# A hybrid attention and RWKV-7 backbone: the next front's VectorE work behind the transposes of the running inversion, and two modulation units made in another stage

## The chip, the core and the metric

The kernel runs on one core of one Trainium2 chip. Its engines are TensorE (PE; PEld is its weight load), VectorE (DVE), ScalarE (ACT), GpSimd (POOL) and SyncE (SP, whose queue issues the DMAs here). The metric is the device time of one launch in microseconds (us), as the median of several runs; beside it there is one execution taken by the hardware profiler, from which all rows below come.

## The reference

Two layers over a trunk of 256 context tokens and 512 latent tokens, 1024 features, in float32. Every sub-layer is normalised, and shifted, scaled and gated by vectors that a linear map makes out of SiLU(c) for latent tokens and SiLU(c_ctx) for context tokens (adaLN):

```
sh1, sc1, gt1, sh2, sc2, gt2 = split(silu_c @ ada_w[i] + ada_b[i], 6)    # and the same of silu_cc
h = rmsnorm(x, norm1_g[i]) * (1 + sc1) + sh1
x = x + gt1 * mixer(h)
x = x + gt2 * relu(modulate(rmsnorm(x), sh2, sc2) @ w1)**2 @ w2
```

Layer 0 mixes by windowed grouped-query attention with context keys, a sink per head, QK-norm and rotary positions. Layer 1 mixes by RWKV-7: out of the shifted tokens come r, k, v, a decay w per direction, and a, b; then a generalized delta rule runs over the tokens, forward and backward, 16 heads of 64:

```
S_t = S_{t-1} diag(w_t) + (S_{t-1} a_t) b_t^T + v_t k_t^T ;   y_t = S_t r_t
```

The latent scans start from the last context state of their direction. A group norm, a bonus and a gate per direction, and an output projection follow; then the second MLP.

## The kernel before

**Order of work.** The program is traced stage by stage: setup, attention, MLP of layer 0, features of layer 1, scan, MLP of layer 1. A planner then orders each engine's instructions: it simulates the engines with a cost model and hands each the ready instruction that was traced first. So work that is traced later can stand earlier in an engine's queue when it was ready sooner by the model. On the chip every queue is in order. `issue_after(ins)` adds an edge without a wait: the instructions traced under it, on the engine of `ins`, stand behind `ins` in that engine's queue. Other engines and the DMAs are not bound by it. Loads and stores are all issued by SP.

**adaLN units.** `ada` holds 12 units (six per layer) of 1024 features. A unit is made in two halves (`ada_parts`): eight loads of 128x512 weights (256 KB each), for each four small matmuls (each recorded as two, so 64 records a half) into one PSUM tile of tag "a", then a copy by ACT, a transpose by PE and an addition of the bias by DVE. A half is two parts of four loads. Four halves (units 0 and 1) are made at the start. The other ten units are a list `fill`; in the attention's loop over (head group `gq`, query tile `qt`) two parts of it follow each `attend`, but for four places where a query projection stands instead.

**Features of layer 1** (`rwkv_features`). The tiles hp, xx and kt are placed where the first MLP's tiles stood. DVE makes the normalised tokens (L780), their neighbours' sum (L785) and the mix tiles (L839, L846); PE projects keys out of them (`k_ps`), and row m of `kt` is written when projection m is done. `wtile` loads a weight (L349) and splits it in a high part (ACT or POOL, L330 and L332) and a low part (DVE, L333). `side_weights` does the same with the small matrices; its first loads are the `swr` ones.

**Scan.** The tokens are cut in chunks of 64. Six iterations stand in a list `its`: 0 and 3 are context (four feature tiles of two heads), 1, 2, 4 and 5 latent (two feature tiles). Each goes through these steps:

- `prep(it)`: loads of the features (rings f4 of five buffers, cs of two, en of one), two exponentials by ACT (L1182 and L1183; L1159 and L1160 for context), three or four products by DVE for each feature tile and direction (a "part": L1195, L1196, L1197, L1199), a copy by POOL (L1200), and half of the Gram matrices (`grams`: copies into `pad` by ACT, matmuls L1220, mask by DVE L1226).
- `lanes(it)`: the inversion of the triangular matrices, by 32x32 blocks. Four copies into MT, the transpose L1267, and then 30 dependent steps of products and sums on DVE (L1277, L1280).
- `merge(it)`: the transposes L1285 and L1288 on DVE end the inversion; four copies into GM follow (L1249 on DVE, L1245 on ACT), and two rounds of small matmuls with copies between them (L1295, L1298, L1303, L1306).
- `chain(it)`: the recurrence over the chunks on PE, ACT and DVE (x_ps, u_ps, s_ps, y_ps; DVE's state update is L1405). Its values come by `values` into two z tiles (loads L1337).
- `late(it)`: the other half of the Grams, products by the chunk's decay (L1241) and transposes (L1319), a piece after a chain step.
- `readout(it)`: group norm and gates (L1441 to L1475), a piece after a step of the next chain. Its buffers come from the rings f4 and cs, too.

`front(n)` traces `merge(its[n-1])`, `prep(its[n])` and `lanes(its[n])`. Front 1 comes ahead of the first chain and front n+2 behind chain n. Iterations n and n+2 share one set of AR, BK and GM, so prep(n+2) can write when chain n has read.

Of the kernel before, what the change touches and what calls it, by code (L numbers as in the profile page):

```python
# [1 line left out]

# [6 lines left out]
F32 = mybir.dt.float32  # L9
# [10 lines left out]
P = 128  # L20
# [120 lines left out]
LC = (0, 2, 4, 4)  # L141
NCS = 2
NEN = 1
M0 = 0
SQ = ()
LM = ()
LPRE = 0
# [1 line left out]
TPER = 3  # L149
TPRE = 0  # L150
S1 = 6
AP_ = 2
S3 = 24
C1 = (20,)
C3 = 3
# [13 lines left out]
class K:  # L169
# [46 lines left out]
        self.ada = self.cp.tile([P, 12, 8, 2], F32, name="ada")  # L216


    def ada_parts(self, pool, u, i, tag="adaw", bufs=4, after=None):

        nc = self.nc
        st = {}

        def part(q):
            if q == 0:
                st["ps"] = self.ps.tile([P, 512], F32, tag="a", name="ada_ps")
            ps = st["ps"]
            for k in range(4 * q, 4 * q + 4):
                w = pool.tile([P, 512], F32, tag=tag, bufs=bufs, name="ada_w")
                with self.tc.issue_after(after) if after else ExitStack():  # L230
                    self.last_ada = nc.sync.dma_start(w, self.a["ada_w"][u, i, k]).ins
                for j in range(4):
                    nc.tensor.matmul(ps[32 * j:32 * j + 32, 0:P], self.sil[:, k, :], w[:, P * j:P * j + P],
                                     start=(k == 0), stop=(k == 7), tile_position=(0, 32 * j))
            if q == 0:
                return
            sb = pool.tile([P, P], F32, tag="ada_sb", bufs=2, name="ada_sb")
            nc.scalar.activation(sb, ps[:, 0:P], AF.Copy)
            pt = self.ps.tile([P, 512], F32, tag="a", name="ada_pt")[:, 0:P]
            nc.tensor.transpose(pt, sb, self.ident)  # L240
            f = 8 * u + 4 * i
            nc.vector.tensor_tensor(self.ada[:, u, 4 * i:4 * i + 4], pt.rearrange("p (j x) -> p j x", x=32)[:, :, 0:2],
                                    self.v["ada_b"][:, f:f + 4].unsqueeze(2).to_broadcast([P, 4, 2]), ALU.add)

        return [lambda q=q: part(q) for q in range(2)]
# [145 lines left out]
    def attention(self):  # L391
# [21 lines left out]
        self.sil = rp.tile([P, 8, 32], F32, name="sil")  # L413
        nc.vector.memset(self.sil, 0.0)
        nc.scalar.activation(self.sil[:, :, 0:2], self.cv, AF.Silu)
        wk = []
        for i in range(2):
            for u in (1, 0):
# [6 lines left out]
        first_ada = self.last_ada  # L425
# [170 lines left out]
            query(m)  # L596
        OS = [None] * 4

        fill = [p for u in range(2, 12) for i in range(2) for p in self.ada_parts(rp, u, i, after=first_ada)]
        late = {(0, 1): 4, (0, 3): 5, (1, 3): 6, (1, 5): 7}  # L600
        X = None
        for gq in range(4):
            if gq < 2:
                OS[gq] = slot(f"O{gq}")
            elif gq == 2:
                both = ap.tile([P, 8, T], F32R, tag="hh", name="O23")
                OS[2:4] = [both[:, 0:4], both[:, 4:8]]
                X = self.open_x()
                for k in range(0, 8, 2):
                    nc.sync.dma_start(X[:, k:k + 2], a["xT"][:, k:k + 2])  # L610
            for qt in range(6):
                attend(gq, qt, OS[gq])
                if (gq, qt) in late:
                    query(late[gq, qt])
                else:
                    for _ in range(AP_):
                        if fill:
                            fill.pop(0)()
        for p in fill:
            p()  # L620
        rstack.close()
# [127 lines left out]
    def rwkv_features(self, xs, scan):  # L749
# [64 lines left out]
        def side_weights(src):  # L814

            hi = rp.tile([P, 1024], F32R, tag="swh", name="swh")
            lo = rp.tile([P, 1024], F32R, tag="swl", name="swl")
            for i in range(2):
                c = slice(512 * i, 512 * i + 512)
                raw = tmp(512, "swr")  # L820
                nc.sync.dma_start(raw, src[:, c])
                self.split(raw, hi[:, c], lo[:, c])
            return hi, lo
# [2 lines left out]
        bsel = rload("bsel", F32R).rearrange("p (f m) -> p f m", f=8)  # L826
        cen = rload("cen")
        w_lo = side_weights(a["lw1"])

        def mix_tile(m, k, xh, xl, lat=False, first=False):  # L830
            sl = ML if lat else slice(0, NM)
# [231 lines left out]
    def rwkv_scan(self, xsave, osave):  # L1063
# [174 lines left out]
        def to_end(it, fl, d):  # L1238

            x = it.BK[:, d, fl * it.nch:fl * it.nch + it.nch]  # L1240
            nc.vector.tensor_tensor(x, x, it.PC[:, ::1 - 2 * d, fl, d].unsqueeze(2).to_broadcast([P, it.nch, P]), ALU.mult)  # L1241
# [40 lines left out]
        def merge(it):  # L1282
# [2 lines left out]
            nc.vector.transpose(MT.rearrange("p u i -> p i u"), Lt.rearrange("p t s -> p s t"))  # L1285

            DT = dt if it.n else GM[:, 0, :, 64:96]
            nc.vector.transpose(DT.rearrange("p u t -> p t u"), lane)  # L1288
            R = [slice(64 * d, 64 * d + 32) for d in range(2)]
            Q = [slice(64 * d + 32, 64 * d + 64) for d in range(2)]  # L1290
            for u0 in (0, 16):
# [212 lines left out]
            if nx:  # L1504
                values(*nx)

        yield prep(its[0]) + [lambda fl=fl, d=d: to_end(its[0], fl, d) for fl in range(4) for d in range(2)] + [lambda: turn(its[0]), lambda: lanes(its[0])] + ([lambda: merge(its[0])] if M0 else [])

        self.pst.close()
        self.wst.close()  # L1510
# [21 lines left out]
            return [state[f // 2][:, 0:1], state[f // 2][:, 1:2]]  # L1532

        def front(n):
            if n > M0:
                merge(its[n - 1])
            for p in prep(its[n]):
                p()
            lanes(its[n])
            rest.extend(late(its[n]))  # L1540
            for _ in range(LPRE):
                if rest:
                    rest.pop(0)()
# [215 lines left out]
```

## Time and profile before

| | |
|---|---|
| median of 3 runs | 2294.5 us (2293.07 to 2295.82) |
| the profiled execution | 2292.35 us, of which the span of the trace is 2290.6 us |
| mean granted TensorE clock | 0.931 |
| busy share | PE 90%, PEld 73%, DVE 58%, ACT 37%, POOL 12% |
| stages, roughly | attention's loop to 412 us, its output projection and the MLP of layer 0 to 1029, features to 1375, scan to 1918, MLP of layer 1 to the end |

A row of groups holds: line, engine, operation, tiles (out <- in), shapes, count | busy us, mean ns of one | idle us of the engine just ahead of them, and what ended it. A row of the timeline holds: start, length, engine, line, operation, tiles, count [idle ahead <- what ended it]. A row of waits: who <- whom: total us, times, longest. A row of a table by stretch: from:to, length, then for each engine its busy us (count of instructions), then the granted clock, the share of the DMA engines and GB/s.

### The profile page before, as it was taken

Reading aid. Unit: us, or ns where it says so; the run is one execution under the profiler, and the core shown is the slowest. Engines: PE = TensorE matmul, PEld = TensorE weight load, DVE = VectorE, ACT = ScalarE, POOL = GpSimd, SP = SyncE. Lnnn points to the kernel's source line nnn. Section 1 sums busy time; section 2 is a strip of 40 time slices with the busy share of each in tenths; the row PEclk is TensorE's granted clock in tenths of the full one; section 3 lists DMA queues with packets and bytes.
Section 4 is the critical chain, followed back from the end, with each engine's and each line's share of the span. In section 5 each row is a group of like instructions: output and inputs, shape, how many; then the busy total and the mean of one; then the engine's idle time right before and its main releaser. Section 6 shows DMA issues by size and latency. Waiting matters only on the chain. (4 is left out here: it accounts for less than half of the span.)

```text
span 2290.6 us, 40501 instructions
## 1 busy us (share of the span) xinstructions
PE 2051.4 (90%) x16208; PEld 1669.3 (73%) x16208; DVE 1317.8 (58%) x2736; ACT 857.9 (37%) x1702; POOL 280.5 (12%) x360
## 2 busy tenths in 40 slices
PE   5989999979999999995989798499568896999999
PEld 4876756868888888884867687387457664788887
DVE  4455564363334343349687575888787757445444
ACT  4354454232111111116454446467556543222121
POOL 0122232010000000003010101000110101110110
PEclk8999999989999999997989898698688897999999
DMA  8244465221212122112246434203310312333322
GB/s 292 94 143 141 153 205 158 74 74 65 65 60 65 56 69 61 55 36 90 76 175 226 129 125 155 61 23 95 104 58 14 126 57 74 102 92 99 95 92 79
DMA packets 115886, 229.67 MB, mean 100 GB/s; under 512 B 12913, under 2 KB 31089, under 8 KB 115313
## 3 DMA queue, kind: packets, MB, share of 16 engines
q1 hardware_dynamic: 115696, 227.08, 30.9%
q8 instruction: 128, 2.10, 0.4%
q14 instruction: 62, 0.50, 0.1%
HBM read 191.80 MB, written 32.60 MB: 98 GB/s over the span
## 5 line engine op out<-in xcount | busy, mean ns | idle before, releaser
L333 DVE TENSOR_TENSOR wlo<-wraw,whi 128x1024 fp32r<-128x1024 f32 (+1 forms) x121 | 134.1, 1116 | 322.7 <-ACT whi L330 170.4
L358 PE MATMUL w_ps<-mhh,whi 128*128 128x512 f32 (+1 forms) x768 | 236.0, 362 | 7.3 <-POOL whi L332 4.0
L360 PE MATMUL w_ps<-mhl,whi 128*128 128x512 f32 (+1 forms) x768 | 236.4, 362 | 6.1 <-DVE mhl L313 6.1
L362 PE MATMUL w_ps<-mhh,wlo 128*128 128x512 f32 (+1 forms) x768 | 236.1, 362 | 6.2 <-DVE wlo L333 6.2
L362 PE MATMUL w_ps<-hid,w2l 128*128 128x512 f32 (+1 forms) x768 | 234.0, 359 | 0.0
L360 PE MATMUL w_ps<-hid,w2h 128*128 128x512 f32 (+1 forms) x768 | 231.1, 355 | 0.0
L358 PE MATMUL w_ps<-hid,w2h 128*128 128x512 f32 (+1 forms) x768 | 231.1, 355 | 0.0
L330 ACT ACTIVATE w2h<-w2raw 128x512 fp32r<-128x512 f32 x64 | 40.4, 632 | 329.9 <-PE w_ps L360 297.9
L332 POOL TENSOR_SCALAR whi<-wraw 128x1024 fp32r<-128x1024 f32 (+1 forms) x60 | 70.0, 1167 | 675.0 <-PE w_ps L360 252.9
L654 DVE SCALAR_TENSOR_TENSOR X<-w_ps,ada,X 128x256 f32<-128x256 f32 (+1 forms) x128 | 73.1, 613 | 137.6 <-PE w_ps L362 137.6
L362 PEld LDWEIGHTS w_ps<-mhh,wlo 128*128 128x128 f32 x768 | 128.1, 190 | 32.7 <-DVE wlo L333 9.4
L358 PEld LDWEIGHTS w_ps<-mhh,whi 128*128 128x128 f32 x768 | 128.2, 190 | 31.9 <-POOL whi L332 4.8
L360 PEld LDWEIGHTS w_ps<-mhl,whi 128*128 128x128 f32 x768 | 128.1, 190 | 32.1 <-DVE mhl L313 8.7
L358 PEld LDWEIGHTS w_ps<-hid,w2h 128*128 128x128 f32 x768 | 127.4, 189 | 23.3
L330 ACT ACTIVATE whi<-wraw 128x1024 fp32r<-128x1024 f32 (+1 forms) x61 | 59.1, 968 | 224.7 <-PE w_ps L360 103.8
L362 PEld LDWEIGHTS w_ps<-hid,w2l 128*128 128x128 f32 x768 | 126.5, 188 | 20.8
L360 PEld LDWEIGHTS w_ps<-hid,w2h 128*128 128x128 f32 x768 | 125.5, 188 | 21.9
L683 ACT ACTIVATE mrelu<-w_ps 128x768 f32<-128x768 f32 (+1 forms) x64 | 44.5, 697 | 190.4 <-PE w_ps L362 190.3
L1220 PE MATMUL g_ps<-pad,bk 128*128 128x128 f32 x640 | 96.6, 301 | 3.3 <-ACT pad L1217 2.4
L332 POOL TENSOR_SCALAR w2h<-w2raw 128x512 fp32r<-128x512 f32 x64 | 42.0, 657 | 426.2 <-PE w_ps L360 326.7
L559 DVE CUSTOM_DVE_ANT_0 sm<-sc_ps,consts,vecs 128x256 f32<-128x256 f32 (+2 forms) x96 | 71.7, 760 | 39.1 <-PE pt_ps L580 19.9
L1220 PEld LDWEIGHTS g_ps<-pad,bk 128*128 128x128 f32 x640 | 83.5, 206 | 12.0 <-ACT pad L1217 5.6
(373 smaller groups left out, 4554.1 us busy)
## 6 DMA issues: line engine op xcount, KB each, us to landing
ada_w<-ada_w SPq DMA_DIRECT2D x192, 256.0 KB, 3.6
wraw<-w SPq DMA_DIRECT2D x64, 512.0 KB, 3.2
w2raw<-w SPq DMA_DIRECT2D x128, 256.0 KB, 2.6
feat<-cs SPq DMA_DIRECT2D x16, 390.0 KB, 2.4
cs<-feat SPq DMA_DIRECT2D x24, 260.0 KB, 2.9
wraw<-wq SPq DMA_DIRECT2D x8, 512.0 KB, 3.6
wraw<-wo SPq DMA_DIRECT2D x8, 512.0 KB, 3.2
wraw<-wkv SPq DMA_DIRECT2D x8, 512.0 KB, 3.3
```

Of the source, the lines that this page charges most:

```text
L330: nc.scalar.activation(hi, raw, AF.Copy)
L332: nc.gpsimd.tensor_scalar(hi, raw, 1.0, 0.0, ALU.mult, ALU.add)
L333: nc.vector.tensor_tensor(lo, raw, hi.bitcast(F32), ALU.subtract)
L358: nc.tensor.matmul(o, wh, cut(xh, sl), start=start, stop=False)
L360: nc.tensor.matmul(o, wh, cut(xl, sl), start=False, stop=False)
L362: nc.tensor.matmul(o, wl, cut(xh, sl), start=False, stop=stop)
L559: nc.vector.tensor_tensor_reduce(sm[:, :nk], ps[:, :nk], self.c["band"][:, b0:b0 + nk], rs[:, h:h + 1], self.v["sink"][:, hd:hd + 1], ALU. ...
L654: self.nc.vector.scalar_tensor_tensor(self.X[:, m, sl], ps[:, sl], self.ada[:, u, m, s:s + 1], self.X[:, m, sl], ALU.mult, ALU.add)
L683: nc.scalar.activation(r, ps[:, 0:n], AF.Relu)
L1220: nc.tensor.matmul(g[:, P * k:P * k + P], it.BK[:, d, b + k], pv[:, :, k], start=True, stop=True)
```

## The change

1. `merge` keeps its second transpose (L1288) as `it.back`. `front(n)` traces `prep(its[n])` under `issue_after(its[n-1].back)`: all DVE instructions of prep(n) stand behind that transpose on DVE's queue. Its loads, its exponentials on ACT, its POOL copies and its matmuls are not bound.
2. Units 8 and 9 (gate 1 and shift 2 of layer 1) leave `fill` and are made in `rwkv_features`, behind the first `side_weights`, ahead of the first mix. Their weights go through nine buffers that are cut out of `kt[:, 1:7]`, their `sil` and their copies stand in `kt[:, 7]`, and POOL writes that `sil` (a memset and a copy). For this, DVE copies SiLU(c) back into `cv` at the start.
3. The remaining 32 parts of `fill` are spread evenly over the 20 places of the attention's loop (12 times two, then 8 times one).
4. Constants that were not used otherwise (M0 of zero, AP_) go.

```
-    def ada_parts(self, pool, u, i, tag="adaw", bufs=4, after=None):
+    def ada_parts(self, pool, u, i, tag="adaw", bufs=4, after=None, home=None):
+        sil = home[0] if home else self.sil
...
-                w = pool.tile([P, 512], F32, tag=tag, bufs=bufs, name="ada_w")
+                w = next(home[1]) if home else pool.tile([P, 512], F32, tag=tag, bufs=bufs, name="ada_w")
...
-            sb = pool.tile([P, P], F32, tag="ada_sb", bufs=2, name="ada_sb")
+            sb = next(home[2]) if home else pool.tile([P, P], F32, tag="ada_sb", bufs=2, name="ada_sb")
...
+        nc.vector.tensor_copy(self.cv, self.sil[:, :, 0:2])
...
-        fill = [p for u in range(2, 12) for i in range(2) for p in self.ada_parts(rp, u, i, after=first_ada)]
+        fill = [p for u in EARLY for i in range(2) for p in self.ada_parts(rp, u, i, after=first_ada)]
+        steps = 24 - len(late)
...
-                    for _ in range(AP_):
-                        if fill:
-                            fill.pop(0)()
+                    steps -= 1
+                    for _ in range(-(-len(fill) // (steps + 1))):
+                        fill.pop(0)()
...
         w_lo = side_weights(a["lw1"])
+        sil = kt[:, 7, 0:256].rearrange("p (k x) -> p k x", k=8)
+        nc.gpsimd.memset(sil, 0.0)
+        nc.gpsimd.tensor_copy(sil[:, :, 0:2], self.cv)
+        wsl = kt[:, 1:7].rearrange("p a t -> p (a t)")
+        home = (sil, itertools.cycle([wsl[:, 512 * i:512 * i + 512] for i in range(9)]),
+                itertools.cycle([kt[:, 7, 256 + P * i:256 + P * i + P] for i in range(2)]))
+        for u in LATER:
+            for i in range(2):
+                for p in self.ada_parts(None, u, i, home=home):
+                    p()
...
-            nc.vector.transpose(DT.rearrange("p u t -> p t u"), lane)
+            it.back = nc.vector.transpose(DT.rearrange("p u t -> p t u"), lane).ins
...
         def front(n):
-            if n > M0:
-                merge(its[n - 1])
-            for p in prep(its[n]):
-                p()
+            merge(its[n - 1])
+            with tc.issue_after(its[n - 1].back):
+                for p in prep(its[n]):
+                    p()
             lanes(its[n])
```

with EARLY = (2, 3, 4, 5, 6, 7, 10, 11) and LATER = (8, 9).

More of the change, by code (lines that the diff above doesn't have):

```diff
@@ L1 @@
+import itertools
 from contextlib import ExitStack
@@ L143 @@
 NEN = 1
-M0 = 0
 SQ = ()
@@ L151 @@
 S1 = 6
-AP_ = 2
+EARLY = (2, 3, 4, 5, 6, 7, 10, 11)
+LATER = (8, 9)
 S3 = 24
@@ L232, in part @@
                 for j in range(4):
-                    nc.tensor.matmul(ps[32 * j:32 * j + 32, 0:P], self.sil[:, k, :], w[:, P * j:P * j + P],
+                    nc.tensor.matmul(ps[32 * j:32 * j + 32, 0:P], sil[:, k, :], w[:, P * j:P * j + P],
                                      start=(k == 0), stop=(k == 7), tile_position=(0, 32 * j))
@@ L1505, in lookahead @@
                 values(*nx)
-        yield prep(its[0]) + [lambda fl=fl, d=d: to_end(its[0], fl, d) for fl in range(4) for d in range(2)] + [lambda: turn(its[0]), lambda: lanes(its[0])] + ([lambda: merge(its[0])] if M0 else [])
+        yield prep(its[0]) + [lambda fl=fl, d=d: to_end(its[0], fl, d) for fl in range(4) for d in range(2)] + [lambda: turn(its[0]), lambda: lanes(its[0])]
         self.pst.close()
```

## The prediction

> **What bounds the kernel now.** First the 40 slices of 57 us, to find where TensorE is not full:
>
> ```profile
> PE   5989999979999999995989798499568896999999
> DVE  4455564363334343349687575888787757445444
> ```
>
> The attention and the MLPs are PE's (nines). Two regions aren't: slices 18 and 20 to 23 (the features) and 24 to 31 (the scan, 1375 to 1800 us). Next the waits in the scan:
>
> ```profile
> PE mg L1295 <- DVE mt L1285: 59.1, 3, 29.4
> ACT gm L1245 <- DVE dt L1288: 41.5, 4, 19.1
> ```
>
> PE stands 59 us in three waits for the transposes that end an inversion. The inversion is a chain of dependent instructions on DVE, begun by L1267 and ended by L1285 and L1288. One of them on DVE's timeline:
>
> ```profile
> 1429.54 1.97 DVE L1267 STREAM_TRANSPOSE lane<-mt 128x1024 f32<-128x1024 f32 x1
> ...
> 1444.64 0.68 DVE L1196 TENSOR_TENSOR bk<-l_bp,en 128x512 f32<-128x512 f32 x1
> 1445.24 0.68 DVE L1195 TENSOR_TENSOR bk<-l_kp,en 128x512 f32<-128x512 f32 x1
> ...
> 1454.56 0.69 DVE L1196 TENSOR_TENSOR bk<-l_bp,en 128x512 f32<-128x512 f32 x1 [2.77 <-DMA l_bp<-feat]
> ...
> 1460.10 0.68 DVE L1199 TENSOR_TENSOR ar<-l_r,cs 128x512 f32<-128x512 f32 x1
> ...
> 1477.15 2.00 DVE L1285 STREAM_TRANSPOSE mt<-lane 128x1024 f32<-128x1024 f32 x1
> 1479.05 1.87 DVE L1288 STREAM_TRANSPOSE dt<-lane 128x1024 f32<-128x1024 f32 x1
> ```
>
> L1195 to L1199 are the next front's products (prep(2)). They stand between the steps of the inversion of front 1, and where one waits for a load (2.77 us) the inversion waits too. Cut at the starts of L1267 and L1285, the scan is five pairs of "inversion" and "after", the first from 1429.54:
>
> ```profile
> 1429.54:1477.15 47.61, 19.33 (x265) 16.58 (x263) 44.35 (x181) 19.84 (x44) 5.70 (x8) 0.73 0.25 73
> 1477.15:1504.15 27.00, 23.45 (x413) 21.58 (x414) 13.18 (x18) 17.77 (x37) 0.00 (x0) 0.71 0.01 2
> 1504.15:1550.93 46.78, 41.23 (x694) 35.02 (x692) 44.26 (x192) 31.55 (x100) 6.44 (x14) 0.96 0.16 47
> 1550.93:1588.40 37.47, 34.79 (x522) 27.25 (x524) 32.14 (x54) 28.75 (x60) 0.69 (x3) 0.78 0.29 86
> 1588.40:1644.45 56.05, 34.70 (x564) 25.34 (x560) 51.87 (x199) 30.77 (x85) 8.50 (x12) 0.74 0.39 116
> 1644.45:1672.70 28.25, 24.71 (x438) 22.64 (x438) 14.32 (x19) 19.19 (x38) 0.88 (x2) 0.73 0.08 28
> 1672.70:1724.85 52.15, 26.00 (x413) 22.55 (x412) 46.66 (x189) 22.40 (x51) 9.34 (x11) 0.80 0.23 72
> 1724.85:1751.00 26.15, 22.59 (x413) 20.81 (x414) 13.22 (x19) 17.81 (x38) 0.00 (x0) 0.74 0.01 3
> 1751.00:1791.10 40.10, 38.41 (x663) 32.90 (x661) 38.63 (x175) 27.31 (x89) 4.37 (x8) 1.00 0.08 22
> ```
>
> Columns: stretch, its length, busy PE, PE loads, DVE, ACT, POOL, then clock and DMA. DVE fills the inversions (44 of 48, 52 of 56) and has room in the "after" ones, where PE and ACT work. The last inversion has no front behind it, takes 40.1 us with the same steps, and PE runs through it: it is the control. So in the scan DVE's order sets the end.
>
> **The change, part 1: the products behind the transposes.** Nothing is removed; the DVE instructions of prep(2) to prep(5) move behind L1288. Prep(1) ran behind its transposes already. How many were inside the inversions, and the idle in front of them, from DVE's groups by shape, 1429.54 to 1724.85:
>
> ```profile
> L1196 DVE TENSOR_TENSOR bk<-l_bp,en 128x512 f32<-128x512 f32 x12 | 8.2, 685 | 7.2 <-ACT en L1182 3.5 <-DMA l_bp<-feat 2.8 <-PE s_ps L1394 0.9
> L1195 DVE TENSOR_TENSOR bk<-l_kp,en 128x512 f32<-128x512 f32 x12 | 8.2, 685 | 1.5 <-ACT en L1182 1.3
> L1197 DVE TENSOR_TENSOR ar<-l_kk,cs 128x512 f32<-128x512 f32 x12 | 8.2, 681 | 0.0
> L1199 DVE TENSOR_TENSOR ar<-l_r,cs 128x512 f32<-128x512 f32 x11 | 7.5, 681 | 1.1 <-PE y_ps L1419 1.1
> L1195 DVE TENSOR_TENSOR bk<-l_kp,en 128x256 f32<-128x256 f32 x8 | 3.3, 409 | 1.1 <-ACT en L1159 1.1
> ```
>
> 47 wide ones at 0.60 from start to start (1444.64 to 1445.24) are 28.2 us. Of the 24 narrow ones of prep(3) (three lines, eight each; two like the last row) 18 stand before 1550.93, at 0.34 from 8/3.3 overlapped: 6.1. Idle in front of them: 7.2 + 1.5 + 1.1 + 1.1 = 10.9. **Gross: 45 us** off four inversions (the fourth pair's 52.15 would come to 40, as the control has it).
>
> What comes back lies in the "after" stretch. Room of DVE there: 27.00 - 13.18 = 13.8, 5.3, 13.9 and 12.9 us, against about 9.6 for a latent prep. So the work fits, except for prep(3), whose stretch PE nearly fills as well (34.79 of 37.47). But prep isn't only work: its 16 instructions took from 1444.64 to 1460.8, 16.2 us, paced by the exponentials into the single en buffer and by the loads of its second feature, issued on SP when the first has let its buffers go. These now start only when DVE gets there. The deadline is PE's grams:
>
> ```profile
> 1479.30 3.62 PE L1295 MATMUL mg<-mt,gm 32*32 32x32 f32 x128 [29.39 <-DVE mt L1285]
> ...
> 1487.88 2.08 PE L1220 MATMUL g_ps<-pad,bk 128*128 128x128 f32 x8
> ...
> 1505.37 0.29 PE L1415 MATMUL y_ps<-gm,z 128*64 128x64 f32 x4
> 1502.12 0.69 DVE L1226 TENSOR_TENSOR gm<-g_ps,s_gmask 128x512 f32<-128x512 f32 x1 [0.66 <-PE g_ps L1220]
> ```
>
> Grams of prep(2) stood ready and yet ran at 1487.88, 10.7 us behind L1285, since PE's queue has the merge ahead of them; the last was masked at 25 us. After the change prep begins at 3.8 (both transposes) + 1.4 (two copies of the merge) = 5.2, its first part is done at 7.6 and its last at 5.2 + 16.2 = 21.4; the last part's copies and matmuls need about 3 more. That is level with the old pace, with nothing to spare. What is late next is the start of the next inversion. Bounds per latent front: 0 (hidden) to 16.2 (all in line). I take 3, being nearest to the room shown: 9 for three. Prep(3) finds 5.3 us of room for 6.1 of moved work and a full PE: bounds 0 to 8 (its moved work and wait), I take 7. The exponentials of three parts (ACT en, cs) fall among the merge's ACT copies; ACT idles 27.00 - 17.77 = 9.2 us there, so 1 each, 4. **Scan: 45 - 9 - 7 - 4 = 25 us faster.** Loads and z tiles share SP's queue; that is a rival below. If the cover were gone, all of the 45 would come back.
>
> **Part 2: four unit-halves leave the attention.** 256 matmuls, 4 transposes, 4 copies, 4 adds and 32 loads of 256 KB.
>
> ```profile
> L233 PE MATMUL ada_ps<-ada_w,sil 128*32 128x128 f32 x1120 | 56.2, 282 | 6.6 <-DMA ada_w<-ada_w 6.3
> 46.66 1.95 PE L233 MATMUL ada_ps<-ada_w,sil 128*32 128x128 f32 x64
> 150.00:412.00 262.00, 253.38 (x2503) 175.84 (x2502) 141.78 (x384) 122.49 (x309) 66.73 (x94) 0.99 0.52 162
> ```
>
> PE is busy 253.38 of 262, so what leaves it shortens the stretch. A half costs 1.95 at its tightest and (56.2 + 6.3) x 64 / 1120 = 3.6 on average with its waits: 7.8 to 14.3 for four. Some of it filled the softmax's latency, so I take 10. One may lose all of that filling: lower bound 4.
>
> **Part 3: they come into the features.** PE waits there while DVE makes the mix tiles:
>
> ```profile
> 1053.37 1.01 PE L358 MATMUL k_ps<-mxh,whi 128*128 128x512 f32 x2 [18.34 <-ACT mxh L843]
> 1034.79 1.02 SPq L821 DMA_DIRECT2D swr<-lw  x2
> 1039.94 11.55 POOL L332 TENSOR_SCALAR swh<-swr 128x512 fp32r<-128x512 f32 x1 [11.35 <-DMA swr<-lw]
> 0.00:50.00 50.00, 28.39 (x331) 21.31 (x331) 23.65 (x43) 19.26 (x32) 3.15 (x6) 0.90 0.85 303
> ```
>
> The 18.34 us wait holds 4 x 1.95 = 7.8 of matmuls. But 8.4 MB at the 303 GB/s of the kernel's start are 28 us; queued behind the swr loads they run from 1036 to 1064, past 1053. So two halves fall into the key projection, 4 us of PE; the loads of its next weights stand behind them on SP. DVE, full there, may stand at one of the four adds if the planner puts it too early. Bounds: 0 to 13 (PE or DVE held until 1066). PE lost 2 to 3 us there by itself, so I take 3. The copy of cv, memset and copy on POOL: POOL is idle from 1028.6 to 1039.9, under 1 us, free.
>
> The same copy of 128x512 takes POOL 657 ns elsewhere; from 1035.5 on DVE works without a break:
>
> ```profile
> L332 POOL TENSOR_SCALAR w2h<-w2raw 128x512 fp32r<-128x512 f32 x64 | 42.0, 657 | 426.2 <-PE w_ps L360 326.7
> ```
>
> The Trainium skill (GPSIMD Engine Reference, section Specifications) says that GpSimd's SBUF interface is shared with VectorE and contended by DVE instructions with two SBUF inputs. By it the new memset, were it queued behind 1035.5, would take some 11 us and hold all the new matmuls: part 3 would be 13, the forecast 2272. The trace agrees with the rule, at that one instruction.
>
> A second rule, TensorE: Matmul & The Clock Gate, section What's actually happening, halves the clock after an idle window of about 3.4 us. The first k_ps pairs (1.01 where later ones have 0.51) agree. By it a PE kept busy before 1053 starts them warm, a gain of 2 to 3 us at most; the scan's waits stay longer than the window, so nothing there.
>
> **Sum.** The profiled execution took 2292.35 us (span 2290.6), 2.15 under the median of 2294.5. 25 + 10 - 3 = 32 us off: 2260.4, and 2262.5 on the median's scale.
>
> **Rivals.**
> (B) More than I forecast: the fronts hide fully (45) and the attention gives 14, since readout(2), whose buffers prep(4) shares, leaves the inversion too and makes up for prep(3). 2294.5 - 45 - 14 + 3 = 2238. For it: the room of 13 us. Against: prep's 16.2.
> (C) Moved only: each inversion is shorter and the next starts that much later, since the grams wait for prep. Scan 0 to 5 faster, with 7 for the units: 2285. For it: the deadline is met with nothing to spare.
> (D) Slower, by SP's queue:
>
> ```profile
> SPq L1337 <- PE y_ps L1415: 147.2, 10, 52.9
> ```
>
> SP, in order, stands up to 52.9 us before a z load, which waits until the running chain has used the older z tile. If such a load is issued ahead of the loads of prep's second feature, these land only behind L1415 of the second chain step (1505.37, 28.2 behind L1285), plus 3: parts 3 and 4 end at 36 instead of 21.4, and each of four inversions begins 15 later: 60, with the 16 of the other losses 76 against 45. 2294.5 + 31 - 7 = 2318. Scan and attention have 52 to give and lose 16 already, so it decides from some 10 us of delay per front on ((52 - 16 + 4.6) / 4). Against it: the wait of 147.2 is there now and prep's loads get through.
> (E) It does nothing: the units cost in the features what they save, and prep(2) to (5) can't start earlier than now for other reasons. 2294. Against: the order on DVE is seen in the rows.
>
> **Chances.** Forecast 0.53 (own range 2247 to 2278), B 0.12, C 0.18, D 0.10, E 0.07. About 0.2% (4.6 us) is what a measurement can tell from no change. Faster: forecast, B and most of C, 0.80; same: E and the rest of C, 0.10; slower: D, 0.10. The range of 2236 to 2290 takes in the forecast, C and most of B; D, E and the rest of B are left out, 0.2.
>
> **What would show it.** In the changed kernel's timeline no L1195 to L1199 between L1267 and the next L1285; the four inversions near 40 to 46 us; "after" stretches of 27 to 32, with DVE fuller. PE's wait for L1285 falls from 59 to under 30. Attention ends some 10 us earlier; L233 rows stand between 1030 and 1060 and the first k_ps comes within 3 us of its old distance. It is wrong if the "after" stretches grow by as much as the inversions shrink (C), if L1196 waits for its loads over 10 us (D), or if PE's wait before k_ps grows (part 3).

## The result and the profile after

| | before | changed |
|---|---|---|
| median | 2294.19 us (4 runs) | 2269.32 us (2264.83 to 2270.0, 4 runs) |
| ratio to before, 95% interval | | 0.9884 (0.987 to 0.9898) |
| the profiled execution, and its span | 2292.35, 2290.6 | 2270.0, 2268.2 |
| mean granted TensorE clock | 0.931 | 0.944 |

The change makes the kernel 24.9 us faster; 32 were forecast (2262.5), and the time lies in the range. In the scan a line of the changed kernel has the old number plus 18 (L1267 is L1285, L1285 is L1303, L1288 is L1306, L1195 to L1199 are L1213 to L1217).

The scan by stretch, cut at the starts of the two transposes as before (columns as in the prediction's table):

```profile
1427.80:1463.18 35.38, 18.36 (x277) 16.18 (x275) 35.18 (x165) 13.85 (x33) 2.32 (x5) 0.80 0.06 17
1463.18:1498.95 35.77, 27.74 (x447) 25.50 (x448) 23.57 (x35) 24.68 (x52) 2.02 (x3) 0.67 0.28 83
1498.95:1538.02 39.07, 37.48 (x633) 32.01 (x631) 37.72 (x173) 25.80 (x84) 3.59 (x8) 1.00 0.08 23
1538.02:1577.41 39.39, 32.00 (x546) 26.09 (x547) 34.14 (x64) 31.46 (x67) 3.05 (x8) 0.87 0.36 102
1577.41:1613.56 36.15, 29.14 (x549) 23.07 (x546) 33.44 (x170) 20.78 (x70) 4.44 (x9) 0.99 0.23 68
1613.56:1652.18 38.62, 31.29 (x515) 26.59 (x516) 32.19 (x46) 30.90 (x62) 2.67 (x5) 0.79 0.38 112
1652.18:1695.29 43.11, 24.37 (x355) 20.10 (x353) 40.80 (x179) 17.48 (x39) 3.53 (x7) 0.84 0.17 50
1695.29:1726.57 31.28, 24.98 (x447) 22.87 (x448) 23.56 (x36) 23.53 (x50) 2.02 (x3) 0.73 0.29 86
1726.57:1766.31 39.74, 37.92 (x639) 32.25 (x635) 38.39 (x173) 26.93 (x86) 4.37 (x8) 1.00 0.09 23
```

The first four inversions take 35.38, 39.07, 36.15 and 43.11 us where they took 47.61, 46.78, 56.05 and 52.15: 48.9 off, and 0.4 off the last. The four "after" stretches take 35.77, 39.39, 38.62 and 31.28 where they took 27.00, 37.47, 28.25 and 26.15: 26.2 more. DVE's work only changed places: in the second row it has 23.57 us of it instead of 13.18.

DVE's groups by shape, 1427.8 to 1695.3 of the changed kernel, answer to the groups that the prediction counted:

```profile
L1217 DVE TENSOR_TENSOR ar<-l_r,cs 128x512 f32<-128x512 f32 x8 | 5.4, 681 | 1.6 <-DMA l_r<-feat 1.6
L1213 DVE TENSOR_TENSOR bk<-l_kp,en 128x512 f32<-128x512 f32 x8 | 5.4, 678 | 3.4 <-ACT en L1200 3.4
L1215 DVE TENSOR_TENSOR ar<-l_kk,cs 128x512 f32<-128x512 f32 x8 | 5.4, 678 | 4.3 <-ACT cs L1201 4.3
L1214 DVE TENSOR_TENSOR bk<-l_bp,en 128x512 f32<-128x512 f32 x8 | 5.4, 675 | 0.0
```

The products take what they took (0.68 us). What ends DVE's idle time in front of them is now mostly ACT's two exponentials (3.4 and 4.3 us in two latent fronts) and less often a load (1.6); an exponential can itself have waited for a load, as a row below shows. The stretch table for L1213 alone shows that none is left inside an inversion; two inversions with the stretches between (columns: stretch, length, DVE busy, clock, DMA share, GB/s):

```profile
1427.80:1463.18 35.38, 0.00 (x0) 0.80 0.06 17
1463.18:1498.95 35.77, 2.71 (x4) 0.67 0.28 83
1498.95:1538.02 39.07, 0.00 (x0) 1.00 0.08 23
1538.02:1577.41 39.39, 3.32 (x8) 0.87 0.36 102
```

Now the waits of the scan, with L1303 and L1306 for the old L1285 and L1288:

```profile
ACT gm L1263 <- DVE dt L1306: 51.4, 5, 21.6
...
PE mg L1313 <- DVE mt L1303: 44.8, 4, 19.4
```

PE's longest wait for the end of an inversion fell from 29.4 to 19.4 us. The total of 44.8 takes in all of the scan, where the kernel before has 60.1 in four waits; in the stretches of the table alone it fell from 59.1 to 43.4 us, three waits each, while ACT's wait for the second transpose grew from 41.5 to 49.8. The next view is ACT's timeline in the second row of the table, the stretch that grew by 8.8 us:

```profile
1469.12 1.19 ACT L1316 ACTIVATE mt<-mg 32x512 f32<-32x512 f32 x2
1470.34 0.63 ACT L1200 ACTIVATE en<-cs 128x512 f32<-128x512 f32 x1
1470.88 1.68 ACT L1235 ACTIVATE pad<-ar 64x256 f32<-64x256 f32 x4
1472.57 1.19 ACT L1316 ACTIVATE mt<-mg 32x512 f32<-32x512 f32 x2
...
1476.85 1.19 ACT L1324 ACTIVATE gm<-mg 32x512 f32<-32x512 f32 x2
1479.96 0.63 ACT L1200 ACTIVATE en<-cs 128x512 f32<-128x512 f32 x1 [1.93 <-DMA cs<-feat]
...
1483.48 0.57 ACT L1390 ACTIVATE xsb<-x_ps 64x128 f32<-64x128 f32 x2
```

Prep's exponential and its four pad copies (2.2 us) stand between two copies of the merge; the merge's last copy begins 13.7 us behind L1303, and the last part's exponential waits 1.93 us for a load with the chain's first copy (xsb, ACT's copy of x_ps) queued behind it. PE's own waits in this stretch show what that delays:

```profile
PE u_ps L1397 <- ACT xsb L1390: 2.9, 1, 2.9
PE mg L1321 <- ACT mt L1316: 2.9, 2, 1.5
```

PE, in order, stands 2.9 us for that copy at a step of the chain, with Grams of the next front behind it in its queue, and 2.9 us for the merge's copies, where the same stretch of before had 1.4.

The features. PE's two rows, then one row of DVE and two of POOL:

```profile
1031.51 4.88 PE L237 MATMUL ada_ps<-kt 128*32 128x128 f32 x64 [3.24 <-DMA kt<-ada_w]
1043.51 3.35 PE L237 MATMUL ada_ps<-kt 128*32 128x128 f32 x64 [6.24 <-DVE ada L246]
1046.78 0.98 PE L362 MATMUL k_ps<-mxh,whi 128*128 128x512 f32 x4
```

```profile
1037.20 6.18 DVE L791 TENSOR_TENSOR xx<-hp 128x770 f32<-128x770 f32 x7
1043.30 0.16 DVE L246 TENSOR_TENSOR ada<-ada_pt,vecs 128x8 f32<-128x8 f32 x1
```

```profile
1023.05 0.35 POOL L838 MEMSET kt<- 128x256 f32 x1 [23.60 <-DVE nacc L286]
1023.46 0.20 POOL L839 COPY kt<-cv 128x16 f32<-128x16 f32 x1
```

The first half waits for its weights, the second for the addition of the first, which stands on DVE behind the neighbours' sums (L791). The other two halves run at 1054.35 and 1065.07 inside the key projection.

A table of stages, from the timelines of the profiled executions, serves for all runs below. Its cuts are the first and the last w_ps matmul of the first MLP, and the first and the sixth transpose L1285 (L1303 or L1304 in the other kernels).

| kernel | to the MLP | MLP | features | scan | rest |
|---|---|---|---|---|---|
| before | 474.2 | 553.7 | 347.4 | 415.8 | 499.5 |
| changed | 469.1 | 551.2 | 352.3 | 393.8 | 501.9 |
| changed, again | 471.7 | 552.2 | 350.6 | 393.5 | 498.4 |
| order alone | 474.1 | 553.7 | 346.9 | 395.3 | 500.0 |
| units alone | 469.0 | 552.2 | 349.8 | 415.0 | 502.3 |
| control of the temporaries | 466.9 | 552.2 | 351.6 | 393.9 | 499.0 |
| three cs buffers | 467.7 | 553.7 | 351.0 | 385.5 | 498.4 |
| two en buffers | 461.0 | 553.7 | 351.3 | 387.8 | 499.0 |
| two en buffers, again | 465.2 | 552.6 | 352.4 | 387.6 | 498.4 |
| three cs, two en, four f4 | 470.9 | 552.2 | 351.4 | 392.2 | 500.6 |
| first part free | 468.7 | 551.1 | 349.1 | 391.6 | 499.0 |
| two en, first part free | 466.3 | 552.1 | 350.2 | 401.3 | 502.2 |
| units 8, 9 left out | 470.3 | 552.2 | 348.5 | 392.5 | 504.8 |
| four units moved | 461.2 | 553.7 | 361.6 | 389.4 | 497.2 |

Where two rows have the same scan (changed, again, control), its time agrees within 0.4 us. The time to the first MLP is less steady: 461.0 to 471.7 us with the same two units moved.

### The profile page after: what moved, and what is told of

Its sections match the earlier page's. It is cut to its first block, busy times and chain, and to the rows that moved or that the text cites. A ratio compares the mean times of both kernels' runs of the same rounds, so it can differ in the third digit from the quotient of the medians.

```text
span 2268.2 us, 40460 instructions
## 1 busy us (share of the span) xinstructions
PE 2049.9 (90%) x16208; PEld 1668.3 (74%) x16208; DVE 1320.1 (58%) x2737; ACT 857.2 (38%) x1702; POOL 263.7 (12%) x362
## 5 line engine op out<-in xcount | busy, mean ns | idle before, releaser
L334 ACT ACTIVATE whi<-wraw 128x1024 fp32r<-128x1024 f32 (+1 forms) x61 | 59.1, 968 | 222.7 <-PE w_ps L364 100.8
L337 DVE TENSOR_TENSOR w2l<-w2raw,w2h 128x512 fp32r<-128x512 f32 x128 | 89.1, 697 | 4.8 <-ACT w2h L334 4.6
```

What stands on the lines that cost most here:

```text
L334: nc.scalar.activation(hi, raw, AF.Copy)
L337: nc.vector.tensor_tensor(lo, raw, hi.bitcast(F32), ALU.subtract)
```

## The experiments

The theory was that the scan's gain is the order's alone, and that what came back is the pace of prep behind the transposes. Its rivals: the merge on ACT and PE sets the pace; the units carry more of the gain, or cost more, than forecast.

**The order alone** (the kernel before, with the edge).

```
         def front(n):
             merge(its[n - 1])
-            for p in prep(its[n]):
-                p()
+            with tc.issue_after(its[n - 1].back):
+                for p in prep(its[n]):
+                    p()
```

> The kernel before with the order edge alone (prep behind L1288), the units left in the attention. By the two traces the scan from the first to the last L1285 became 22.0 us shorter (415.9 to 393.8). If the two parts of the change are independent, this kernel takes 2294.2 - 22 = 2272, with four inversions near 35, 39, 36 and 43 us. If a part of the 22 us came by way of the units (other times of the loads, another order by the planner from the features on), it takes more than 2276.

Measured: 2271.74 us against 2295.77, ratio 0.9898 (0.988 to 0.9916): 24 us. The scan loses 20.5 of 415.8, all other stages stay within 0.6. The four inversions take 35.4, 39.8, 34.7 and 47.1 us, 45.5 less than before, and the stretches behind them 25.7 more.

```profile
1464.02:1494.65 30.63, 24.31 (x412) 21.97 (x413) 22.91 (x35) 24.01 (x49) 2.01 (x3) 0.70 0.33 97
1494.65:1534.47 39.82, 38.68 (x666) 33.13 (x666) 38.32 (x175) 26.38 (x87) 3.57 (x8) 1.00 0.08 22
...
1694.79:1730.24 35.45, 27.02 (x447) 24.93 (x448) 23.59 (x35) 23.51 (x50) 2.02 (x3) 0.68 0.25 76
```

The same order of DVE gives stretches of different length: the first is 30.63 us here and 35.77 in the changed kernel, the last 35.45 here and 31.28 there. PE's waits tell them apart. In the two long ones it stands 2.9 us for ACT's xsb (changed kernel, above) and, here in the last, for a mask:

```profile
PE g_ps L1220 <- DVE gm L1226: 3.3, 1, 3.3
PE mg L1303 <- ACT mt L1298: 2.9, 2, 1.5
```

In the two short ones the waits for xsb are 0.2 and 1.1 us, and the wait for the merge's copies is the same 2.9. So 4 to 5 us of each long stretch go with the place of one chain step between the Grams on PE's queue, which the planner sets: in the changed kernel the first stretch holds 447 matmul records and here 412. Prep's end doesn't explain them: in the repeated run of the changed kernel it came at 18.6 instead of 19.9 us in the first stretch, which took 35.9 us with the same wait of 2.9.

**The units alone** (the changed kernel without the edge).

```
-            with tc.issue_after(its[n - 1].back):
-                for p in prep(its[n]):
-                    p()
+            for p in prep(its[n]):
+                p()
```

> The changed kernel without the order edge: the units alone. By the two traces the attention ended 5.1 us earlier, the MLP of layer 0 took 2.5 less, and the features gave 4.8 of it back: 2291.5 if all three are the change's doing. If the MLP's 2.5 and the features' loss are chance of one execution, 5.1 stand: 2289. By the prediction's own terms (10 and 3) 2287.

Measured: 2287.7 us, ratio 0.9962 (0.9948 to 0.9976), 8 us. The stages don't show all of it: in the profiled execution, the slowest of the six (2290.02 us), they come to 2.4 us less than before, and by the means of all kernels with these two units moved to 3.9 (worked out in the section on the prediction). The scan is the old one:

```profile
1424.59:1471.88 47.29, 19.18 (x265) 16.32 (x263) 44.33 (x180) 20.14 (x44) 6.18 (x8) 0.75 0.25 74
1471.88:1498.05 26.17, 22.64 (x413) 20.78 (x414) 13.16 (x18) 17.78 (x37) 0.00 (x0) 0.74 0.01 3
```

The two parts alone sum to 32 us, together they gave 24.9 and (below) 27; with 3 to 6 us of uncertainty on each that is no interaction that could be shown.

**Three cs buffers.** One more buffer for the loads of a part; to make room, the inversion's temporaries stand in MT.

```
-NCS = 2
+NCS = 3
...
+            spare = MT.rearrange("p u i -> p (u i)")
...
-                    tmp = sa.tile([P, (120, 200, 80)[i]], F32, tag=f"lt{i}", name="ltmp")[:, :m * n].rearrange("p (t i) -> p t i", t=m)
+                    tmp = spare[:, 256 * i:256 * i + m * n].rearrange("p (t i) -> p t i", t=m)
```

> The changed kernel with three cs buffers instead of two (the small temporaries of the inversion moved into MT, which nothing uses then, to make room). Theory 1, the ring paces: in the changed trace ACT stands for the load of the fourth decay row (1.9 us) ahead of the chain's copies, and DVE idles 2.2 and 2.1 us for it; with a third buffer each of the three latent after-stretches loses 3 to 4 us, 2269 - 10 = 2259. Theory 2, the work itself is the cost (DVE's 9.9 us, ACT's exponentials between the merge's copies): no change, 2267 to 2271.

Measured: 2258.64 us, 0.9839 (0.9821 to 0.9856).

**Two en buffers** (NEN = 2 and the same move of the temporaries).

> The changed kernel with two en buffers instead of one (same room made). Theory 1, the cs ring paces: the exponential can go ahead of DVE by one part, but the decay rows still come late; at most 1 us a stretch, 2266 to 2269. Theory 3, the single en buffer paces, as the prediction had it: 3 us a stretch, 2260.

Measured: 2257.2 us, 0.9832 (0.9815 to 0.9849).

**The changed kernel again, and the control** (rings as in the changed kernel, only the temporaries moved).

> The changed kernel once more, on the chip of the three that follow, so that they have a common measure. If the two parts of the change add up as they did alone (24.0 for the order and 8.1 for the units), 2295 - 32 = 2263; if the first measurement holds and the parts take from each other, 2269.

> The control of the two runs with wider rings: the changed kernel with the inversion's temporaries in MT and the rings as they were. Theories 1 and 3 (the rings' width gave the 11 and 12 us): within 3 us of the changed kernel. Rival (the planner orders the scan otherwise as soon as anything is moved, and the gains are its luck, or the temporaries' place is the gain): 2257 to 2261, as with the wider rings.

Measured: 2266.31 us, 0.9871 (0.9845 to 0.9896), and 2265.59 us, 0.9871 (0.9847 to 0.9895). The repeat lies between its two expectations and decides neither. The move of the temporaries is worth nothing, so what is gained comes with the ring's edit: the scan goes from 393.9 to 385.5 us with three cs buffers and to 387.8 with two en buffers. The stretches behind the first and the fourth of these inversions, with three cs buffers:

```profile
1461.56:1491.62 30.06, 24.32 (x412) 21.97 (x413) 22.87 (x35) 24.02 (x49) 2.02 (x3) 0.69 0.34 99
...
1687.98:1717.72 29.74, 23.80 (x412) 21.69 (x413) 22.86 (x34) 22.86 (x47) 2.01 (x3) 0.71 0.28 82
```

Neither has the long wait (PE's wait for xsb in the first is 0.2 us). What is left over the old 27.00 and 26.15 is 3.1 and 3.6 us, near what the prediction had for a latent front. But the three latent stretches did not lose 3 to 4 us each, as was expected: against the changed kernel they lose 5.7, nothing (38.71 for 38.62) and 1.5. The first is the place of the chain step again, since the order alone has 30.63 us there with two cs buffers. The planner orders the scan anew when a ring changes, and the control, whose rings are the old ones, can't part this from the ring's width. For the second en buffer the pace itself is seen: prep's last product ends 15.8 to 16.5 us behind the transpose in both measurements instead of 18.6 to 20.4, and the third and fourth stretches take 36.3 to 36.9 and 28.3 to 28.5 us instead of 38.6 and 31.3.

**All rings wider at once** (NCS = 3, NEN = 2, and NF4 = 4 to make room).

> Both rings wider (three cs, two en) and, to make room, four f4 buffers instead of five. If cs and en pace one after the other, prep in the latent after-stretches ends 2 us earlier than with either alone (15.8 behind L1285 with two en) and the time is 3 to 5 us under e4_nen2, 2253; if the loads of the second feature (f4) are what is left, they come later now and the time is not under 2258.

Measured: 2260.58 us (2257.58 to 2269.06), 0.9855 (0.9824 to 0.9885); its scan takes 392.2 us, more than with either ring alone. That is one execution, the slowest of four; 59.4 us of it stand ahead of the first inversion (53.5 and 56 to 57 with one ring). The f4 buffer that was given for it is the difference in the edit; which wait carries it was not isolated.

**The first part free** (the changed kernel, each prep's first part ahead of the edge).

```
+            parts = prep(its[n])
+            parts.pop(0)()
             with tc.issue_after(its[n - 1].back):
-                for p in prep(its[n]):
+                for p in parts:
```

> The changed kernel with the first part of each prep left free of the order edge: 4 products (2.4 us, with a wait at times) go back into each inversion, and the rings move on by one part ahead of the transposes. If the after-stretches are paced by prep's end (18.6 to 20.4 behind L1285), they lose 3 to 4 us each, against 2.4 more in the inversions: the same time within 4 us. If prep's end doesn't matter, four times 2.4: 10 us slower than the changed kernel.

Measured: 2262.14 us, 0.9863 (0.9833 to 0.9893): not told from the changed kernel by time; the scan takes 391.6 instead of 393.8. Inversions are 2 to 3 us longer again, the "after" stretches shorter.

**Two en buffers and the first part free.**

> The changed kernel with a second en buffer (as in the run with two en buffers, the inversion's temporaries standing in MT) and with the first part of each prep outside the order edge. If the 26 us that the stretches behind the transposes gave back are prep's own pace (its start behind L1288 and its single en buffer), the two add up: the ring alone gave 8 us, the free part some 2, so 2255 us, 0.9825. If the stretches are set by then by ACT's merge copies and PE's grams, the free first part gives nothing more: 2257, 0.9835. If the first part's products in the inversion cost more than they give (about 2.4 us of DVE in each of four), 2262, 0.9855.

Measured: 2272.18 us, 0.9895 (0.9878 to 0.9911), by the ratios 9 to 14 us above the two measurements of two en buffers alone: worse than each expectation, with the direction of the last. An inversion and the stretch behind it:

```profile
1425.26:1463.52 38.26, 18.78 (x267) 16.21 (x265) 37.03 (x168) 16.11 (x37) 5.47 (x7) 0.81 0.08 23
1463.52:1494.21 30.69, 23.97 (x412) 21.87 (x413) 20.55 (x31) 21.32 (x43) 0.60 (x1) 0.68 0.30 88
```

DVE has 2.7 us less to do in the stretch than with two en buffers alone (23.29, below), prep's last product ends 14.5 us behind the transpose instead of 16.0, and the stretch is 30.69 against 30.88. So by now prep doesn't set the end of this stretch. The scan is 13.7 us longer than with two en buffers: the inversions take 8.7 of it (2.6 in the row above), since the free parts stand in them, and the stretches behind the transposes 5.0, of which only the sum is shown.

**Two en buffers again.**

> The kernel with two en buffers once more, since its first profiled execution had an attention 8 us shorter than the others of the same order and since the run with the free first part (2272.18 us) stands 15 us above it. If the ring itself gives the scan 6 us (387.8 us from the first transpose to the last, against 393.8 in the changed kernel) and the free first part took them back, 2259 to 2261 us, 0.984 to 0.986. If the first measurement was mostly the short attention, 2264 to 2268, 0.987.

Measured: 2259.8 us, 0.9856 (0.9836 to 0.9876). The scan repeats, 387.6 after 387.8 us; the stretch that answers to the one above:

```profile
1426.54:1462.22 35.68, 18.31 (x267) 16.03 (x265) 35.23 (x165) 13.41 (x31) 2.60 (x6) 0.78 0.06 17
1462.22:1493.10 30.88, 24.48 (x415) 21.46 (x416) 23.29 (x36) 24.41 (x50) 1.19 (x2) 0.75 0.31 96
```

The kernel with the wider ring has 6 us less of scan, both times; the rest of its first lead was a shorter time to the first MLP (461.0 us in that execution).

**Units 8 and 9 left out** (the changed kernel without the four halves; their place in ada is filled with zeros).

```
-LATER = (8, 9)
+LATER = ()
...
+        nc.vector.memset(self.ada[:, 8:10], 0.0)
```

> The changed kernel with units 8 and 9 not made at all (the four halves are left out in the features, and their slots of ada hold zeros), so its output isn't the reference's. It prices part 3: the changed kernel runs beside nothing else but these four halves' 256 matmuls, 32 loads, 4 transposes and 4 adds. By the prediction's term the features gain 3 us and the kernel comes 3 us below the changed one (ratio to the kernel before 0.986). By what the traces of the changed kernel showed (the stretch from the last key projection to r_ps 2.6 us longer, v_ps 2.4 us later against the attention's gain of 5) it is 2 to 3 us; if the features hide the halves wholly, 0. If the additions that wait in DVE's queue cost the mix tiles more than the trace's rows say, 6 us or more.

Measured: 2270.24 us, 0.9887 (0.987 to 0.9904): nothing gained in the total. In the features alone it is 348.5 us against 349.1 to 352.4 of the ten kernels that make two units there (mean 351.0). What moved in its trace, PE and then POOL:

```profile
1047.14 1.01 PE L363 MATMUL k_ps<-mxh,whi 128*128 128x512 f32 x2 [18.34 <-ACT mxh L862]
1050.42 1.01 PE L363 MATMUL k_ps<-mxh,whi 128*128 128x512 f32 x2 [2.27 <-POOL whi L337]
```

```profile
1034.96 10.31 POOL L337 TENSOR_SCALAR swh<-swr 128x512 fp32r<-128x512 f32 x1 [8.19 <-DMA swr<-lw]
1045.24 5.12 POOL L337 TENSOR_SCALAR whi<-wraw 128x512 fp32r<-128x512 f32 x1
```

The long wait of 18.34 us is back, as before the change, and POOL's copy takes 10.31 us again, with the key's first weights (whi) behind it and PE waiting 2.27 us for them. With the units there, the swr load comes later (1044.42) and the copies take 1.38 and 1.31 us. So the halves take some time from the features and give some back. The rest behind the scan is 504.8 us here, 4.9 above the mean of those ten, which hides the 2.5 in the total; what makes it longer was not isolated.

**Four units moved** (units 8 to 11).

```
-EARLY = (2, 3, 4, 5, 6, 7, 10, 11)
-LATER = (8, 9)
+EARLY = (2, 3, 4, 5, 6, 7)
+LATER = (8, 9, 10, 11)
```

> The changed kernel with two more units (10 and 11, eight halves in all) moved from the attention to the features. If a half is worth in the attention what the prediction took (2.5 us) and costs in the features 0.75 us, another 7 us go: 0.985. If a half is worth 1.2 us, as the attention's 5 us for four say, and costs 0.6 to 1.2, it comes out level: 0.987 to 0.989. If the features have no more room for another 8.4 MB of weights, which would stand ahead of the key projection's own weights on SP's queue, 10 us or more slower: 0.992.

Measured: 2264.26 us (2256.66 to 2266.76), 0.9854 (0.9831 to 0.9877), not told from the changed kernel. In its profiled execution it takes 461.2 us to the first MLP, 13 less than before for eight halves, and 361.6 in the features, 14 more. Against the means of the kernels with two units moved (467.9 and 351.0) the second four halves gained 6.7 and gave back 10.6. The 6.7 come from one execution, and kernels with four halves moved spread from 461.0 to 471.7 in that stage, so they are not shown; the 10.6 lie well outside the 349.1 to 352.4 of the features.

**What beats both kernels:** three cs buffers (2258.64 us) or two en buffers (2257.2 and 2259.8 us) on top of the change, 33 to 39 us under the kernel before.

## Why the prediction was right, and where its terms were off

The sum was 25 + 10 - 3 = 32 us. Counted the same way in the stages: scan 22.0 (415.8 to 393.8); to the first MLP 6.3, and 1.4 in it, as means over the eleven executions in which these two units, and no others, are gone from the attention; features 3.8 lost, as the mean of ten against that of the two kernels that make no unit there (347.2). 22.0 + 6.3 + 1.4 - 3.8 = 25.9, against 24.9 and 27.0 measured. The 1.4 in the MLP may be chance: three of the kernels with units moved have 553.7 us there, as before. That the scan's 22 came near the 25 is partly luck, since three errors of the terms below nearly cancel: 3.9 more left the inversions, 12.3 more came back in the latent fronts, and 6.1 less in prep(3)'s.

**The bound was read rightly.** The products were inside the inversions, none is now, and the order alone carries 20.5 us of the scan with the other stages untouched. The last inversion, with no front behind it, was a fair control: the first four come to 35 to 43 us where it took 40.1. Of the signs that were named, two inversions fell below the 40 to 46 us (35.38 and 36.15), and two of the three latent stretches rose above the 27 to 32 (35.77 and 38.62).

**The gross, 45, was 48.9** (45.5 with the order alone). The third inversion fell by 19.9 us, and readout(2) left it too: the readouts' DVE time inside, counted from start to start, is 4.6 us, the end of readout(1), instead of 11.6, nearly all readout(2). The prediction had this as rival B's reason alone.

**What comes back, 20, was 27.2** (26.2 in the four stretches and 1.0 in the one ahead of them, 54.3 to 55.3; 25.7 in the four with the order alone): the mis-sized term. By front it stood at 3 + 1 for each latent one and 7 + 1 for prep(3). Measured: 8.8, 10.4 and 5.1 for the three latent ones, 1.9 for prep(3). Prep's own pace was right: its last product ended 18.6 to 20.4 us behind the transpose, for 21.4 forecast. Four things were not in the step:
- The step let prep run up to the last Gram mask, 25 us behind the transpose, as if the Grams of its first parts could be masked meanwhile. But the masks, too, are on DVE's queue and stand there behind nearly all of the products: in the latent fronts the first one comes at 18.1 to 19.9 us instead of 12.8 to 12.9. Rows of the fourth stretch, the first from the kernel before:

```profile
1737.69 0.69 DVE L1226 TENSOR_TENSOR gm<-g_ps,s_gmask 128x512 f32<-128x512 f32 x1 [7.63 <-PE g_ps L1220]
```

```profile
1713.18 0.68 DVE L1217 TENSOR_TENSOR ar<-l_r,cs 128x512 f32<-128x512 f32 x1
1713.79 1.27 DVE L1244 TENSOR_TENSOR gm<-g_ps,s_gmask 128x512 f32<-128x512 f32 x2
...
1726.57 1.97 DVE L1285 STREAM_TRANSPOSE lane<-mt 128x1024 f32<-128x1024 f32 x1
```

Here the mask's delay is all of the growth: from the first mask to the next inversion it takes 12.8 us, against 13.3 before. With two en buffers the first mask comes at 15.7 us and the same way takes 12.8 again, a stretch of 28.5 instead of 31.3.
- The merge's copies share ACT's queue with prep's exponentials and pad copies. In the latent fronts the merge's last copy ends at 14.8 instead of 12.0 us behind the transpose, and the chain's first copy begins at 18.4 to 20.3 instead of 15.8 to 16.7. The prediction had 1 us for this. With prep shortened by a ring and a free part (its last product at 14.5) the merge's last copy ends at 16.1 in the first stretch, and 3.7 us of growth stay there (30.69 against 27.00).
- In the first stretch PE's wait for xsb and the chain step that stands with it make up the rest of the 8.8: without it the same stretch takes 30.63. This is read from kernels that differ in more than this wait; no edit changed it alone.
- The readouts moved against the cuts. By the sum over their lines, counted in the same way, readout(1) has 7.1 us of DVE in prep(3)'s stretch instead of 11.5, so that prep(3)'s 6.3 more found room and the 7 forecast for it fell away; and readout(2) has 6.6 us in the third stretch, where 0.7 of readout(1) stood, which goes with the 5.3 that this stretch grew more than the fourth, and 5.0 instead of none in the fourth inversion, which stayed at 43.11. No run moved the readout alone; with the order alone it has 5.1 there, and that inversion takes 47.1, so the readout isn't the whole reason.

**PE's wait for the inversion's end** fell by 10 us in the longest case, and the total from 59.1 to 43.4, not under 30: a miss in size. The chain reaches its end sooner than the inversion does in two fronts still (18.92 and 19.4 us).

**Attention, 10, was 6.3 (7.7 with the MLP).** A half is worth 1.6 us there and not 2.5; the run with eight halves moved agrees, as far as one execution tells (13 / 8). It is below the tight half of 1.95; without the uncertain 1.4 of the MLP the term's lower bound of 4 was the nearer one. Where the lost part goes, for the changed kernel (the attention's loop is the same in work but for the halves):

```profile
150.00:407.00 257.00, 246.16 (x2252) 172.93 (x2251) 142.61 (x381) 121.49 (x305) 67.96 (x97) 0.98 0.42 132
```

PE is busy 7.2 us less, but it idles 10.8 us instead of 8.6: this reads as some of the halves having filled waits of the softmax, as the step allowed for; no run showed it apart.

**Features, 3, was 3.8, or 2.5 against the one execution without the units.** POOL's memset and copy were free, and two halves fall into the key projection, as written. DVE did not stand at an addition: PE stood 6.24 us at one that was late. The first k_ps came 26.5 us behind the MLP's last matmul instead of 25.5, within the 3 us. Part of the loss is later: from the last k_ps to the first r_ps 21.3 us instead of 18.8, with PE's wait for POOL (tile sg) up from 5.3 to 7.0; the run without the units has 19.2 there, with 6.5 of that wait, so why it is longer is open.

**The two rules.** The first concerns POOL's work beside DVE's. POOL ran the memset at 1023.05, ahead of DVE's unbroken work, so its rival case, 11 us, didn't come, and no run shows a memset beside such work. The copy took 11.55 us before and 10.31 without the units, and ended both times 0.5 us behind the last of DVE's neighbour sums, two-input operations; in the changed kernel its load landed as these ended, and it took 1.38 us, beside one more such operation. This agrees in kind with the Trainium skill (GPSIMD Engine Reference, section Specifications), by which GpSimd's interface to SBUF is shared with VectorE and contended by instructions with two SBUF inputs. The second concerns the clock. In the 2 us behind the first k_ps the granted clock was 0.50 before; in the 1.2 us behind it in the changed kernel it was 1.00, and four k_ps records take 0.98 us, where two took 1.01. This agrees with the Trainium skill (TensorE: Matmul & The Clock Gate, section What's actually happening), by which an idle window halves the clock. The key projection is 0.6 us shorter (107.9 against 108.5), although two halves, 3.9 us of PE, now stand in it.

**The rivals.** B's mechanism came in part (readout(2) left the third inversion, and a part of it went into the fourth), without its size. C's did too: between the second transpose and the third nothing was gained (73.8 to 74.8 us, -7.7 in the inversion, +8.8 ahead of it); the gain sits in the stretches from the first to the second (101.9 to 90.6) and the third to the fourth (93.5 to 75.5), while the fourth to the fifth (80.4 to 81.7) and the fifth to the sixth (66.2 to 71.0) lose 6. With the order alone the second to the third gains 3.3 and the fourth to the fifth loses 5.3, so where the gain sits depends on the planner's order. D's loads made DVE wait 1.8 us in all and ACT 1.9 and 0.9 us at two exponentials, not 10 a front. E is excluded by the order alone.

## What to carry to other kernels

When independent work is moved off a serial chain in an in-order queue, cut the loop at the chain's ends and price both halves: here 49 us left the chain and 27 came back beside it. Count for the moved work what it needs on the other engines' queues (here ACT's exponentials between the merge's copies) and on its own engine's queue (here the masks behind the products). One more buffer in a ring of one or two went with a scan 6 to 8 us shorter, a part of which is another order of the chain's steps. Work that fills another engine's waits can be worth less than its tightest time when it leaves: here 1.6 us for a half of 1.95, as a mean of eleven executions against two.

## What was not expected of the hardware

- GpSimd's copy of 128x512 took 11.55 and 10.31 us while DVE ran two-input operations without a break, and 1.38 when its load came as these ended. A copy that began 9.5 us later ended at nearly the same time (1045.8 in the changed kernel, 1045.3 without the units).
- A half of 64 small matmul records took 4.88 us behind an idle stretch of PE, at a granted clock of 0.50 and with weights landing between its groups of eight; 3.35 behind the next wait, at 0.56; and 1.96 in a busy stretch, at 1.00.
- The stages differ in how well they repeat: the scan of one order within 0.4 us, the time up to the first MLP within a spread of 11 us (461.0 to 471.7).
